# Feed-forward networks of a two-layer decoder as 2x2 blocks with seven products in place of eight

## The chip, the cores and the metric

The kernel runs on one core of one Trainium2 chip. The metric is device time in microseconds, from the first to the last instruction of the core, for one launch. TensorE (PE in the profile, PEld for its loading of the stationary side) multiplies matrices; VectorE (DVE), ScalarE (ACT) and GpSimd (POOL) work on elements; SyncE (SP) issues the transfers. Every engine takes its instructions in the order in which they stand in its own queue, and an instruction at the head that waits holds up all behind it.

## The reference

Two layers on 1024 tokens of 1024 values. Layer 0 mixes tokens by a gated delta rule, layer 1 by stick-breaking attention; behind each mixer stands a SwiGLU feed-forward network of 2816 columns. The change is in these two networks.

```python
def swiglu(x, w_gu, w_down):
    g, u = jnp.split(x @ w_gu, 2, axis=-1)
    return (jax.nn.silu(g) * u) @ w_down

    for layer in range(DEPTH):
        hn = rms_norm(h, attn_norm[layer])
        ...
        h = h + swiglu(rms_norm(h, ffn_norm[layer]), ffn_w_gu[layer], ffn_w_down[layer])
```

In float32. The kernel splits each side of a product into a high and a low part (float32r) and adds three products: high x high, high x low, low x high.

## The kernel before

The stream h lies in SBUF as eight tiles of 128 tokens x 1024. The tail of a mixer adds its output product to h by blocks (`final_put`, L329) and gives each finished row block to `Norm`: `tile` (L205 to L211) scales the row, `half` transposes half of the tokens (four 128x128 transposes a column block, L222) and splits the result to the high and low right sides `xT` (ACT L230, DVE L231). The first four row blocks are one half of the tokens, the other four the second half.

`ffn` (L334) goes over 22 column units of 128 columns, in groups of two or three. Of a unit, gate and up are two stationary matrices of 1024 x 128: `col_raw` (L111) loads one, 512 KB, `split` casts it (ACT, L102) and subtracts (DVE, L103). `proj_half` (L139 to L141) runs for each half of the tokens over 8 row blocks of the weights x 3 parts, 24 matmuls 128x512 into one PSUM bank. `gate` applies Silu (ACT, L344), `up` multiplies (DVE, L348) and splits the hidden values (ACT L351, DVE L352); these stay in SBUF. After a group, `row_unit` (L126) has loaded and split its rows of w_down, and `down_steps` (L256 to L258) makes the 16 blocks of 128 tokens x 512 columns, three matmuls a unit, each added to h by DVE (L329). In the first unit the products by the second half of the tokens wait for `norm.half()`, and the first half's stand ahead of it (`proj_two_steps`).

Loads are issued by SP in program order, as buffers come free (`raw` has 3, weights `w` 4). No order is written out by hand in these stages: program order is that of the code, and each engine waits only on the buffers and the data. The changed `ffn` below keeps the names of pools: `w` is the pool of weights in `main`, `n` the pool of row tiles with 4 buffers, `ips` and `ups` PSUM banks.

## Time and profile before

| | |
|---|---|
| time, median of 3 runs | 2762.84 us (2760.97 to 2763.07) |
| the profiled execution's own span | 2763.6 us, mean granted clock 0.996 |
| PE busy | 2691.2 us (97%), 13676 matmuls |
| DVE, ACT, POOL busy | 1392.3 (50%), 903.5 (33%), 531.2 (19%) |
| memory | 157.49 MB by the load and store queue, its packets 18.9% of 16 engines' time; 57 GB/s |
| layer 0's mixer, feed-forward | to 740, about 740 to 1460 |
| layer 1's mixer, feed-forward | about 1460 to 2050, 2050 to 2760 |

The span is that of one profiled execution and is 0.7 us above the median of the timed runs. Busy shares are averages over stages with different limits; what a stage is bound by is read from windows of that stage. A matmul of 512 columns shows a busy time of 0.39 us while the next starts 0.23 us later, since matmuls are pipelined: what one costs is the spacing of the starts.

### The profile page before, as it was taken

The numbers are of one execution on the slowest core, as the hardware profiler recorded it, in microseconds if no ns is written. First come the engines' busy times: TensorE is split into PE (matmuls) and PEld (weight loads), VectorE is DVE, ScalarE is ACT, GpSimd is POOL, SyncE is SP. The second block draws the span as 40 slices with busy tenths as digits, with TensorE's granted clock in tenths as the row PEclk, the third lists the DMA queues.
The fourth block names the chain that finished last, engine by engine and source line by source line (L and its number), as shares of the span: only waits on it lengthen the run. The fifth ranks groups of instructions, "written<-read, shape, count | busy, mean of one in ns | idle before, by whom it ended". The sixth has DMA issues, their size and how long they took to land.

```text
span 2763.6 us, 34344 instructions
## 1 busy us (share of the span) xinstructions
PE 2691.2 (97%) x13676; PEld 2216.1 (80%) x13676; DVE 1392.3 (50%) x2107; ACT 903.5 (33%) x1787; POOL 531.2 (19%) x1044
## 2 busy tenths in 40 slices
PE   8999999999999999999999999999899999999999
PEld 6787778877788888888887788887678888888887
DVE  6666677665633333232245787787743323223223
ACT  5333333342511121011135666667341112101211
POOL 2444444444200000000023334322400000000000
PEclk9999999999999999999999999999999999999999
DMA  4222222223111121121121111112311112102211
GB/s 121 58 63 63 55 61 53 70 93 111 58 50 39 46 69 46 31 61 54 31 99 39 39 31 39 39 47 88 119 38 46 47 38 69 54 23 61 62 28 72
DMA packets 182118, 159.67 MB, mean 58 GB/s; under 512 B 11443, under 2 KB 159038, under 8 KB 181958
## 3 DMA queue, kind: packets, MB, share of 16 engines
q1 hardware_dynamic: 181958, 157.49, 18.9%
q8 instruction: 107, 1.75, 0.3%
q14 instruction: 53, 0.43, 0.1%
HBM read 140.38 MB, written 17.07 MB: 57 GB/s over the span
## 4 chain that ended last, share of the span: by engine, by line
PE 77%; DVE 10%; ACT 4%; issue 4%; POOL 3%; DMA 2%; SPq 0%; POOLq 0%; DVEq 0%; ACTq 0%
PE ups L139 16%; PE ups L140 16%; PE ups L141 16%; PE ups L258 7%; PE ups L257 7%; PE ups L256 7%; DVE l L1005 2%; PE ips L535 2%; DVE wl L103 1%; ACT wh L102 1%; DVE y L502 1%; DMA raw<-in_w_kv_dram 1%; PE ips L222 1%; POOL raw L120 1%; DVE z L1006 1%
## 5 line engine op out<-in xcount | busy, mean ns | idle before, releaser
L139 PE MATMUL ups<-x,wh 128*128 128x512 f32 (+1 forms) x2320 | 936.9, 404 | 0.0
L141 PE MATMUL ups<-x,wl 128*128 128x512 f32 (+1 forms) x2320 | 911.4, 393 | 0.0
L140 PE MATMUL ups<-x,wh 128*128 128x512 f32 (+1 forms) x2320 | 908.1, 392 | 0.0
L141 PEld LDWEIGHTS ups<-x,wl 128*128 128x128 f32 (+1 forms) x2320 | 435.4, 188 | 92.3
L139 PEld LDWEIGHTS ups<-x,wh 128*128 128x128 f32 (+1 forms) x2320 | 436.4, 188 | 77.6
L140 PEld LDWEIGHTS ups<-x,wh 128*128 128x128 f32 (+1 forms) x2320 | 436.7, 188 | 76.1
L103 DVE TENSOR_TENSOR wl<-raw,wh 128x1024 fp32r<-128x1024 f32 x152 | 190.5, 1253 | 407.5 <-ACT wh L102 406.7
L329 DVE TENSOR_TENSOR h<-h,ups 128x512 f32<-128x512 f32 x256 | 175.0, 687 | 255.0 <-PE ups L258 254.9
L102 ACT CAST wh<-raw 128x1024 fp32r<-128x1024 f32 x152 | 159.7, 1051 | 396.4 <-PE ups L140 301.9
L256 PE MATMUL ups<-wdh,hidh 128*128 128x512 f32 x704 | 274.6, 390 | 0.0
L258 PE MATMUL ups<-wdh,hidl 128*128 128x512 f32 x704 | 274.1, 389 | 0.0
L257 PE MATMUL ups<-wdl,hidh 128*128 128x512 f32 x704 | 274.0, 389 | 0.0
L344 ACT ACTIVATE n<-ups 128x512 f32<-128x512 f32 x88 | 52.0, 591 | 517.6 <-PE ups L141 517.5
L120 POOL TENSOR_TENSOR raw<-raw,gains 128x256 f32<-128x256 f32 x96 | 77.6, 836 | 737.1 <-DMA raw<-in_w_kv_dram 709.6
L348 DVE TENSOR_TENSOR n<-n,ups 128x512 f32<-128x512 f32 x88 | 60.5, 688 | 267.2 <-PE ups L141 265.5
L258 PEld LDWEIGHTS ups<-wdh,hidl 128*128 128x128 f32 x704 | 132.2, 188 | 27.5
L257 PEld LDWEIGHTS ups<-wdl,hidh 128*128 128x128 f32 x704 | 132.2, 188 | 27.2
L256 PEld LDWEIGHTS ups<-wdh,hidh 128*128 128x128 f32 x704 | 132.2, 188 | 27.2
L502 DVE SCALAR_TENSOR_TENSOR y<-n,convc,y 128x512 f32<-128x512 f32 x144 | 112.8, 784 | 1.3
L351 ACT CAST hidh<-n 128x512 fp32r<-128x512 f32 x88 | 54.3, 618 | 149.5 <-DVE n L348 149.5
L1005 DVE TENSOR_TENSOR_SCAN l<-l 128x128 f32<-128x128 f32 (+3 forms) x64 | 89.2, 1394 | 22.6 <-POOL l L1001 22.6
L103 DVE TENSOR_TENSOR wdl<-raw,wdh 128x1024 fp32r<-128x1024 f32 x50 | 64.8, 1300 | 65.0 <-ACT wdh L102 65.0
(245 smaller groups left out, 3578.0 us busy)
## 6 DMA issues: line engine op xcount, KB each, us to landing
raw<-in_ffn_w_gu_dram SPq DMA_DIRECT2D x88, 512.0 KB, 3.9
raw<-in_ffn_w_down_dram SPq DMA_DIRECT2D x44, 512.0 KB, 3.5
raw<-in_gdn_w_in_dram SPq DMA_DIRECT2D x32, 512.0 KB, 4.2
ab<-adr SPq DMA_DIRECT2D x128, 64.0 KB, 2.7
raw<-in_w_kv_dram SPq DMA_DIRECT2D x16, 512.0 KB, 3.9
raw<-oT SPq DMA_DIRECT2D x15, 512.0 KB, 3.2
y<-in_x_dram SPq DMA_DIRECT2D x8, 512.0 KB, 7.6
gb<-gcd SPq DMA_DIRECT2D x16, 256.0 KB, 3.7
```

What stands on the lines that cost most here:

```text
L102: act.copy(hi, raw)
L103: dve.tensor_tensor(lo, raw, hi, op=ALU.subtract)
L120: pool.tensor_tensor(raw[:, ks], raw[:, ks], bc(gain[:, ks]), op=ALU.mult)
L139: pe.matmul(o, wh[:, kt, :m], xh, start=kt == 0, stop=False)
L140: pe.matmul(o, wh[:, kt, :m], xl, start=False, stop=False)
L141: pe.matmul(o, wl[:, kt, :m], xh, start=False, stop=kt == KT - 1)
L256: pe.matmul(ps, ah[:, sl], wh[:, ns], start=i == 0, stop=False)
L257: pe.matmul(ps, ah[:, sl], wl[:, ns], start=False, stop=False)
L258: pe.matmul(ps, al[:, sl], wh[:, ns], start=False, stop=i == n - 1)
L329: dve.tensor_tensor(hs, hs if acc is None else acc[t][nh], ps, op=ALU.add)
L502: dve.scalar_tensor_tensor(ys, xr[:, j + sl.start : j + sl.stop], w[j], ys, op0=ALU.mult, op1=ALU.add)
L1005: dve.tensor_tensor_scan(rv, rv, rv, 0.0, op0=ALU.add, op1=ALU.bypass)
```

## The change

Let x be split by halves of the tokens and of the 1024 inputs, and a network's weights alike, so that [C11 C12; C21 C22] = [A11 A12; A21 A22] [B11 B12; B21 B22] needs eight block products. The change computes it with seven, as in Winograd's form of Strassen's scheme, with sums of blocks before and after:

- `PairNorm` (in place of `Norm` ahead of the networks): of the second half of the tokens it makes the right sides T1 to T4 (differences with the first half, by POOL and DVE) and X22, of the first half X11 and X21.
- `Unit`: one column unit has gate and up as the two block rows. Its left sides are the four weight blocks g1, g2 (`split_g`, used in products 1 and 2), u2 (`split22`, product 4) and sums (`sum12`, `sum34` on POOL, for products 5, 6, 3, 7). `Seven.step` runs a product of 12 matmuls (`triple`, L446 to L448) into a bank and then the element work of it (`e1`, `c11`, ...). Products 3 and 4 of a unit follow product 1 of the next one (`ORDER`).
- the hidden values of two units are a 2x2 block of the next product's left side. `sums(q)` makes the sums of pair q on POOL, splits part of them, and `put` stores them to DRAM (`hsa` split, `hsb` as they are) in eleven stores of 256 KB, 512 bytes a piece. The first pair is stored without sums (`sums0`).
- `Right` and `Block`: w_down by pairs of units as right sides, with sums on POOL; the down products by groups of two pairs, seven products of 24 matmuls a block, a block being two tiles of 128 tokens. `Block.plain` makes the first pair by eight products. The sums go to h: by DVE from PSUM (`into`) or by an ACT copy and a POOL add (`via`).
- h is no longer held in SBUF during the column units: `keep_rows` stores its rows to `hmid` and `rows_load` fetches them ahead of the down blocks.

The core of the diff:

```diff
-    def ffn(h, norm, w_gu, w_down, hp, done):
...
-                    proj(norm.xT, col_unit(w_gu, i * P), gate)
-                    proj(norm.xT, col_unit(w_gu, FF + i * P), up)
...
-            run(down_steps(hid, ws, final_put(None, h, done if f == NF else lambda t, nh, ht: None)))
...
+        act.copy(hi, src)
+        dve.tensor_tensor(lo, src, hi, op=ALU.subtract)
+        return hi, lo
...
+            rr = [self.hp.tile([P, 2, HB], F32, tag="W", name="r2", bufs=NW) for _ in range(4)]
+            tt = []
+            for j in range(4):
+                r = rr[j]
+                act.activation(r[:, 0], self.columns(hn, j), AF.Copy, scale=g(j))
+                t1, t2 = x_tile(F32), x_tile(F32)
+                pool.tensor_tensor(t1, r[:, 0], self.raw[j], op=ALU.subtract)
+                act.activation(r[:, 1], self.columns(hn, 4 + j), AF.Copy, scale=g(4 + j))
+                dve.tensor_tensor(t2, r[:, 1], t1, op=ALU.subtract)
+                tt.append((t1, t2))
+            for j in range(4):
+                self.parts("T2", j, tt[j][1])
+            for j in range(4):
+                pool.tensor_tensor(rr[j][:, 0], rr[j][:, 1], rr[j][:, 0], op=ALU.subtract)
+                self.parts("T1", j, tt[j][0])
+            for j in range(4):
+                self.parts("T3", j, rr[j][:, 0])
+                pool.tensor_tensor(rr[j][:, 0], self.raw[4 + j], tt[j][1], op=ALU.subtract)
+            for j in range(4):
+                self.parts("22", j, rr[j][:, 1], self.x2)
+            for j in range(4):
+                self.parts("T4", j, rr[j][:, 0])
...
+        ORDER = (1, -3, -4, 6, 2, 5, 7)
...
+            key, start = {1: ("B", True), 6: ("B", False), 7: ("B", False), 4: ("B", False),
+                          2: ("A", True), 5: ("C", True), 3: ("C", False)}[p]
+            if start:
+                self.bank[i, key] = i_tile((P, HB)) if key == "B" else u_tile()
+            ps = self.bank[i, key]
+            it.products(p, ps, start, p in (2, 3, 4))
+            if p == 2 and not out:
+                return
+            {1: it.e1, 2: it.c11, 6: it.u2, 5: it.p5, 7: lambda q: it.u3(q, self.bank[i, "C"]),
+             4: it.c21, 3: it.c12}[p](ps)
...
+            return hp.tile([P, 2, 4, P], dt, tag="W", name="w", bufs=NW)
...
+            def sum12(self):
+                self.s = W()
+                pool.tensor_tensor(self.s[:, 0], self.u[:, 0], self.u[:, 1], op=ALU.add)
+                pool.tensor_tensor(self.s[:, 1], self.s[:, 0], self.g[:, 0], op=ALU.subtract)
+            def sum34(self):
+                self.r = W()
+                pool.tensor_tensor(self.r[:, 0], self.g[:, 0], self.u[:, 0], op=ALU.subtract)
+                pool.tensor_tensor(self.r[:, 1], self.g[:, 1], self.s[:, 1], op=ALU.subtract)
...
+            def split12(self):
+                self.both(5, 6, self.s, W)
...
+            def split_g(self):
+                self.both(1, 2, self.g, mw)
...
+            def e1(self, ps):
+                self.t1 = ev()
+                act.copy(self.t1, ps)
...
+            def c11(self, ps):
+                self.sg = n_tile()
+                s = self.sg[:, 0:HB]
+                dve.tensor_tensor(s, self.t1, ps, op=ALU.add)
+                act.activation(s, s, AF.Silu)
...
+            def u2(self, ps):
+                self.t2 = ev()
+                act.copy(self.t2, ps)
...
+            def u3(self, ps, c):
+                self.t3 = ev()
+                act.copy(self.t3, ps)
+                dve.tensor_tensor(self.t3, self.t3, c, op=ALU.add)
...
+            def c21(self, ps):
+                s = self.sg[:, 0:HB]
+                dve.tensor_tensor(s, s, ps, op=ALU.mult)
...
+            def c12(self, ps):
+                s = self.sg[:, HB:S]
+                dve.tensor_tensor(s, self.t2, ps, op=ALU.add)
+                act.activation(s, s, AF.Silu)
+                pool.tensor_tensor(s, s, self.t3, op=ALU.mult)
...
+        def put(dst, k, src):
+            sp.dma_start(dst[:, :, k, :].rearrange("c p x -> p c x"), src)
...
+            v = [hid.pop(2 * q + k) for k in range(2)]
+            s = W()
+            pool.tensor_tensor(s[:, 0], v[0][:, :, 1], v[1][:, :, 1], op=ALU.add)
+            pool.tensor_tensor(s[:, 1], s[:, 0], v[0][:, :, 0], op=ALU.subtract)
+            yield
+            r = W()
+            pool.tensor_tensor(r[:, 0], v[0][:, :, 0], v[0][:, :, 1], op=ALU.subtract)
+            pool.tensor_tensor(r[:, 1], v[1][:, :, 0], s[:, 1], op=ALU.subtract)
+            put(hsb[q], 1, v[1][:, :, 1])
+            yield
+            hi = mw()
+            act.copy(hi, s)
+            dve.tensor_tensor(s, s, hi, op=ALU.subtract)
+            put(hsb[q], 0, r[:, 0])
+            put(hsb[q], 2, r[:, 1])
+            yield
+            h2 = mw()
+            for k in range(2):
+                act.copy(h2[:, k], v[k][:, :, 0])
+                dve.tensor_tensor(v[k][:, :, 0], v[k][:, :, 0], h2[:, k], op=ALU.subtract)
+            for k in range(2):
+                put(hsa[q], 2 + k, hi[:, k].bitcast(F32))
+                put(hsa[q], 6 + k, s[:, k])
+            yield
+            for k in range(2):
+                put(hsa[q], k, h2[:, k].bitcast(F32))
+                put(hsa[q], 4 + k, v[k][:, :, 0])
...
+        def rows_load(c):
+            for t in (2 * c, 2 * c + 1):
+                sp.dma_start(h[t], rows[t * P : (t + 1) * P, :])
...
+            def via(self, ps, odd, nh):
+                e = ev()
+                act.copy(e, ps)
+                d = self.half(odd, nh)
+                pool.tensor_tensor(d, d, e, op=ALU.add)
+            def into(self, ps, odd, nh):
+                d = self.half(odd, nh)
+                dve.tensor_tensor(d, d, ps, op=ALU.add)
...
+            def e1(self, ps):
+                self.into(ps, 0, 0)
+            def c11(self, ps):
+                self.into(ps, 0, 0)
+                self.finish(0, 0)
+            def u2(self, ps):
+                self.via(ps, 0, 1)
+            def p5(self, ps):
+                self.into(ps, 1, 1)
+            def u3(self, ps, c):
+                self.via(ps, 1, 1)
+                self.finish(1, 1)
...
+            elif s == 2:
+                if j:
+                    j.split22()
+            elif s == 3:
+                if j:
+                    j.sum34()
+                    if i + 2 < NF:
+                        units[i + 2].load_u()
+                if i % 2 == 0 and i >= 2:
+                    pend.append(sums(i // 2 - 1) if i > 2 else sums0())
+            elif s == 5:
+                if j:
+                    j.split_g()
+            elif s == 6:
+                if j:
+                    j.split12()
+                    if i + 2 < NF:
+                        units[i + 2].load_g()
...
+        run_.step(0, 1)
+        run_.step(0, 2, False)
+        units[1].load_g()
+        units[1].split22()
+        units[1].split_g()
+        run_.step(1, 1)
+        run_.step(1, 2, False)
+        norm.half()
+        for i in range(2):
+            units[i].c11(run_.bank[i, "A"])
+        units[1].sum12()
+        run_.step(0, 6)
+        units[1].sum34()
+        units[2].load_u()
```

Where the instructions stand at the three places that the numbers of the prediction rest on:

PE at the entry of the first network, before: the last transposes of the second half (`n` are the scaled row tiles, `ident` the identity), then the first products by that half (`x` its right sides, `wh` and `wl` the first unit's gate).

```order
L222 MATMUL ips_7748<-ident_69,n_7579 128x128
L222 MATMUL ips_7748<-ident_69,n_7619 128x128
L139 MATMUL ups_7766<-x_7699,wh_7628 128x512 [waits Activation_49]
L222 MATMUL ips_7757<-ident_69,n_7499 128x128 [waits DVE_49]
L222 MATMUL ips_7757<-ident_69,n_7539 128x128
L222 MATMUL ips_7757<-ident_69,n_7579 128x128
L222 MATMUL ips_7757<-ident_69,n_7619 128x128
L140 MATMUL ups_7766<-x_7700,wh_7628 128x512
L141 MATMUL ups_7766<-x_7699,wl_7629 128x512
L139 MATMUL ups_7766<-x_7708,wh_7628 128x512 [waits Activation_49]
L140 MATMUL ups_7766<-x_7709,wh_7628 128x512
L141 MATMUL ups_7766<-x_7708,wl_7629 128x512
```

The same place after the change: the last transposes of the second half, then product 6 of unit 0 (`w` its left side, `x` the right side T2).

```order
L378 MATMUL ips_7827<-ident_69,n_7506 128x128 [waits Activation_49]
L378 MATMUL ips_7827<-ident_69,n_7552 128x128
L378 MATMUL ips_7827<-ident_69,n_7598 128x128
L378 MATMUL ips_7827<-ident_69,n_7644 128x128
L446 MATMUL ips_7701<-x_7834,w_7688 128x512 [waits Activation_49]
L447 MATMUL ips_7701<-x_7835,w_7688 128x512 [waits DVE_49]
L448 MATMUL ips_7701<-x_7834,w_7689 128x512
L446 MATMUL ips_7701<-x_7838,w_7688 128x512 [waits Activation_49]
L447 MATMUL ips_7701<-x_7839,w_7688 128x512 [waits DVE_49]
L448 MATMUL ips_7701<-x_7838,w_7689 128x512
```

The right sides behind the transposes come now from POOL and DVE differences as well; the row blocks' transposes wait for ACT, and each triple of product 6 waits for ACT and DVE.

ACT in a group of column units of the first network, before: `wdh` and `wh` are high parts of weights, `hidh` those of hidden values, `n` the Silu.

```order
L344 ACTIVATE n_9296<-ups_9303 128x512 [waits PE_49]
L102 CAST wh_9618<-raw_9616 128x1024 [waits DMAHW1_49,PE_49,Activation_49]
L344 ACTIVATE n_9296<-ups_9329 128x512 [waits PE_49]
L351 CAST hidh_9387<-n_9296 128x512 [waits DVE_49]
L102 CAST wh_9676<-raw_9674 128x1024 [waits DMAHW2_49,PE_49,Activation_49]
L351 CAST hidh_9417<-n_9296 128x512 [waits DVE_49]
L344 ACTIVATE n_9615<-ups_9622 128x512 [waits PE_49]
L102 CAST wh_9743<-raw_9741 128x1024 [waits DMAHW3_49,PE_49,Activation_49]
```

ACT in an even column unit after the change: `ips` holds the bank of products 1, 6 and 7; the cast of w_9213 (`split12` of the next unit) waits for transfers and POOL, and the cast from raw_9336 and the copy L538 (`u3`) stand behind it.

```order
L521 COPY ev_9211<-ips_9198 128x512 [waits PE_49,Pool_49]
L549 ACTIVATE n_9157<-n_9157 128x512 [waits DVE_49]
L531 COPY ev_9265<-ips_9198 128x512 [waits PE_49]
L358 CAST w_9332<-w_9213 128x1024 [waits DMAHW1_49,DMAHW0_49,Pool_49]
L583 CAST w_9312<-w_9272 128x1024 [waits PE_49]
L527 ACTIVATE n_9288<-n_9288 128x512 [waits DVE_49]
L590 CAST w_9338<-n_9007 128x512 [waits DMAHW7_49,PE_49]
L590 CAST w_9338<-n_9157 128x512
L358 CAST w_9369<-w_9267 128x512 [waits DVE_49,Activation_49]
L358 CAST w_9454<-raw_9336 128x1024 [waits DMAHW3_49,DMAHW5_49,DMAHW2_49,Activation_49]
L538 COPY ev_9329<-ips_9198 128x512 [waits PE_49]
```

Of the casts before, none waits for a store; now `split12` takes a buffer (tag W) that the stores of the pair's sums read.

SP at the passage from column units to down products of the first network, before: loads of the next weights, each as a `raw` buffer comes free.

```order
L111 DMA raw_9297<-in_ffn_w_gu_dram 128x8x128 [waits DMAHW1_49,DVE_49]
L111 DMA raw_9355<-in_ffn_w_gu_dram 128x8x128 [waits DMAHW2_49,DVE_49]
L126 DMA raw_9421<-in_ffn_w_down_dram 128x1024 [waits DMAHW3_49,DVE_49]
L126 DMA raw_9427<-in_ffn_w_down_dram 128x1024 [waits DMAHW6_49,DVE_49]
L126 DMA raw_9433<-in_ffn_w_down_dram 128x1024 [waits DMAHW4_49,DVE_49]
L111 DMA raw_9616<-in_ffn_w_gu_dram 128x8x128 [waits DMAHW7_49,DVE_49]
```

The same queue after the change: the last stores of the last pair, then the loads of the third block's left sides (`hsa` from DRAM, into w_11028 and w_11074).

```order
L553 DMA hsa_7660<-w_10982 128x4x128 [waits DMAHW1_49]
L553 DMA hsa_7660<-w_10953 128x4x128 [waits DMAHW2_49]
L553 DMA hsa_7660<-w_11007 128x4x128 [waits DMAHW3_49,Activation_49]
L553 DMA hsa_7660<-n_10691 128x4x128 [waits DMAHW4_49,DVE_49]
L553 DMA hsa_7660<-w_11007 128x4x128 [waits DMAHW5_49,Activation_49]
L553 DMA hsa_7660<-n_10852 128x4x128 [waits DMAHW6_49,DVE_49]
L664 DMA w_11028<-hsa_7650 128x1024 [waits DMAHW7_49,PE_49]
L687 DMA h_11032<-hmid_7294 128x1024 [waits DMAHW0_49]
L664 DMA w_11074<-hsa_7650 128x1024 [waits DMAHW1_49]
L687 DMA h_11076<-hmid_7294 128x1024 [waits DMAHW2_49]
```

The loads of the third block's left sides stand behind eleven stores that wait for the sums of the last pair.

## Rows read from the trace of the kernel before

**Rows 1.** The page: its head, and busy time, share and instructions of each engine.

```profile
span 2763.6 us, 34344 instructions
PE 2691.2 (97%) x13676; PEld 2216.1 (80%) x13676; DVE 1392.3 (50%) x2107; ACT 903.5 (33%) x1787; POOL 531.2 (19%) x1044
```

**Rows 2.** Busy time of a stretch inside a network; columns are in the first line.

```profile
core 0: us, PE busy (x) PEld busy (x) DVE busy (x) ACT busy (x) POOL busy (x), PEclk, DMA share, GB/s
900.00:1100.00 200.00, 200.00 (x884) 165.69 (x883) 61.42 (x77) 33.22 (x44) 0.00 (x0) 1.00 0.18 53
```

**Rows 3.** Groups by form: busy us, mean ns of one, idle before by releaser.

```profile
L612 POOL TENSOR_TENSOR qd<-y,gb 128x512 f32<-128x512 f32 x16 | 20.7, 1291 | 75.8 <-DVE y L505 38.0 <-PE ips L689 37.1 <-ACT sz L513 0.7
L329 DVE TENSOR_TENSOR h<-h,ups 128x512 f32<-128x512 f32 x256 | 175.0, 687 | 255.0 <-PE ups L258 254.9
L352 DVE TENSOR_TENSOR hidl<-n,hidh 128x512 fp32r<-128x512 f32 x88 | 60.9, 692 | 21.3 <-ACT hidh L351 21.3
L102 ACT CAST wh<-raw 128x1024 fp32r<-128x1024 f32 x152 | 159.7, 1051 | 396.4 <-PE ups L140 301.9 <-issue 85.7 <-DMA raw<-in_ffn_w_gu_dram 5.4
L351 ACT CAST hidh<-n 128x512 fp32r<-128x512 f32 x88 | 54.3, 618 | 149.5 <-DVE n L348 149.5
L344 ACT ACTIVATE n<-ups 128x512 f32<-128x512 f32 x88 | 52.0, 591 | 517.6 <-PE ups L141 517.5
```

**Rows 4.** Single lines: duration ns min/median/max, first and last start us, form.

```profile
L103 DVE TENSOR_TENSOR wl<-raw,wh x152: 1197/1226/2315, 17.6 to 2706.4; 128x1024 fp32r<-128x1024 f32 x152
L321 POOL TENSOR_TENSOR x<-x,n x32: 1277/1301/2298, 675.2 to 1982.9; 128x512 f32<-128x512 f32 x32
L309 DVE TENSOR_TENSOR x<-x,ups x64: 649/686/691, 640.4 to 2007.9; 128x512 f32<-128x512 f32 x64
```

**Rows 5.** The page: transfers, KB each, median us from issue to landing.

```profile
y<-in_x_dram SPq DMA_DIRECT2D x8, 512.0 KB, 7.6
hsp<-h SPq DMA_DIRECT2D x8, 512.0 KB, 2.6
n<-hsp SPq DMA_DIRECT2D x8, 512.0 KB, 3.3
out_dram<-h SPq DMA_DIRECT2D x16, 256.0 KB, 2.0
```

**Rows 6.** Timeline of PE at a network's entry: start, us, instruction, idle before it.

```profile
740.67 3.48 PE L222 MATMUL ips<-ident,n 128*128 128x128 f32 x28
743.90 0.48 PE L139 MATMUL ups<-x,wh 128*128 128x512 f32 x1
744.22 0.60 PE L222 MATMUL ips<-ident,n 128*128 128x128 f32 x4
```

**Rows 7.** Timelines of DVE and of POOL in the mixer's tail, 696 to 701.8.

```profile
696.61 4.30 DVE L103 TENSOR_TENSOR wdl<-raw,wdh 128x1024 fp32r<-128x1024 f32 x2 [0.67 <-ACT wdh L102]
...
697.54 2.29 POOL L321 TENSOR_TENSOR x<-x,n 128x512 f32<-128x512 f32 x1
```

**Rows 8.** Timeline of PE behind two gaps, and the first one's window.

```profile
701.61 0.68 PE L256 MATMUL ups<-wdh,x 128*128 128x512 f32 x1 [2.31 <-issue]
...
702.51 0.63 PE L258 MATMUL ups<-wdh,x 128*128 128x512 f32 x1
702.94 0.63 PE L256 MATMUL ups<-wdh,x 128*128 128x512 f32 x1
...
1972.87 0.50 PE L256 MATMUL ups<-kh,x 128*128 128x512 f32 x1 [2.39 <-DVE x L309]
...
1973.44 0.39 PE L258 MATMUL ups<-kh,x 128*128 128x512 f32 x1
1973.67 0.40 PE L256 MATMUL ups<-qh,x 128*128 128x512 f32 x1
...
700.00:720.00 20.00, 17.74 (x76) 14.28 (x77) 14.59 (x20) 10.18 (x14) 7.96 (x11) 0.91 0.44 130
```

**Rows 9.** The page: the queue's packets, bytes, share of 16 engines' span.

```profile
q1 hardware_dynamic: 181958, 157.49, 18.9%
```

More of the change, by code (lines that the diff above doesn't have):

```diff
@@ new lines, in yoco_kernel, with __init__, x2, columns @@
+    class PairNorm(Norm):
+        def __init__(self, gain, hp):
+            super().__init__(gain)
+            self.hp = hp
+            self.X = {n: [None] * 4 for n in ("11", "21", "T1", "T2", "T3", "T4", "22")}
+            self.raw, self.nhalf = {}, 0
+        def x2(self, dt=F32R):
+            return self.hp.tile([P, HB], dt, tag="x2", name="x2", bufs=NX2)
+        def columns(self, hn, kt):
+            ps = i_tile()
+            for j in range(NTH):
+                pe.transpose(ps[:, j, :], hn[j][:, kt * P : (kt + 1) * P], ident)
+            return ps.rearrange("p a b -> p (a b)")
+        def parts(self, name, j, src, tile_=None):
+            tile_ = x_tile if tile_ is None else tile_
+            self.X[name][j] = parts_of(src, tile_(), tile_())
+        def half(self, n=KT):
+            g = lambda kt: self.gain[:, kt : kt + 1]
+            if self.nhalf == 0:
+                if not self.todo:
+                    self.todo, self.hn = [(self.hn, kt) for kt in range(KT)], []
+                for hn, kt in self.todo[:n]:
+                    r = self.x2(F32)
+                    act.activation(r, self.columns(hn, kt), AF.Copy, scale=g(kt))
+                    self.raw[kt] = r
+                    self.parts(("11", "21")[kt // 4], kt % 4, r, self.x2)
+                self.todo = self.todo[n:]
+                if not self.todo:
+                    self.nhalf = 1
+                return
+            hn, self.hn = self.hn, []
+            rr = [self.hp.tile([P, 2, HB], F32, tag="W", name="r2", bufs=NW) for _ in range(4)]
[20 more added lines that the diff above has]
+                self.parts("T4", j, rr[j][:, 0])
```

380 lines of the change are left out of this document (348 added, 32 removed).

## The prediction

> **What bounds the kernel now.** I read the page first for the shares of the engines: TensorE (PE) is busy for 2691.2 of 2763.6 us [rows 1]. Then the table by stretches, inside the feed-forward networks, which run at about 745 to 1460 and 2050 to 2760: there PE has no idle time at all, at a granted clock of 1.00, with 884 matmuls in 200 us [rows 2], so 0.2262 us a matmul. VectorE (DVE) is busy for 61 of these 200 us, ScalarE (ACT) for 33, GpSimd (POOL) for none. So the networks are bound by the number of matmuls and nothing else. The change takes matmuls away and lays other work on the three idle engines; the sum is what is taken, less what PE then waits for.
>
> **What is taken.** A network holds 22 column units x 2 (gate, up) x 48 = 2112 matmuls for gate and up and 22 x 48 = 1056 for down, 3168. After the change a column unit is seven products of 12 matmuls, so 22 x 84 = 1848; of down, the first pair of units takes eight products (96), the five groups of two pairs take 168 each (840): 2784. That is 384 fewer in a network, 768 in both. The moving side stays 512 wide, so at 0.2262 us this is 173.7 us. All of it lay on the path. The floor, with no new wait, is 2763.6 - 173.7 = 2589.9 us.
>
> **What is added, by engine.** POOL has no 128x512 operation in these stages; the nearest row is L612, 1.29 us. A DVE operation with PSUM is 0.687 us (L329) and with SBUF alone 0.69 (L352); an ACT copy is taken as L344's 0.59, casts are 0.62 (L351) and 1.05 (L102, twice as wide); a wide DVE subtraction is 1.23 [rows 3, 4]. For two column units, 168 matmuls or 38.0 us of PE, this gives POOL 14 x 1.29 = 18 us, DVE 17, ACT 16. For a group of four down blocks, again 38.0 us, DVE has 20 adds from PSUM (13.7) and 13.9 us of subtractions in SBUF, POOL 16 operations (20.6). None exceeds PE. So a loss arises only where one of these queues stands in the wrong order for a moment. I looked for such places in the order of the instructions and found four.
>
> **1. Entry of the network.** Before, the second half's 32 transposes and the first product by it follow one another without a gap [rows 6]. Afterwards that half passes through 12 POOL subtractions and 24 DVE ones before all seven right sides are there. Only four products (10.9 us) need the first half alone. Two parts: (a) the second unit's first product waits for a cast that stands eighth in ACT's queue, behind five casts of 0.62, one of 1.05 and a copy of 0.59, and takes 1.05 itself: 5.8, about 6 us; at best 0, if the casts run while PE is still in the mixer. (b) DVE's 24 subtractions, two adds and a weight's subtraction are 24 x 0.69 + 2 x 0.69 + 1.23 = 19.2 us if POOL (15.5 us) disturbs none of them, 34.7 if every one; PE reaches the sixth product, which needs the last of them, after 13.6 us. So 6 to 21 us, and I take 13, since at most half of POOL's operations can meet them. Entry: 19, between 6 and 27.
>
> **2. Steady column units.** In an even unit, the unit's number being i, the left sides of the pair before are added on POOL, then stored. The chain from the unit's start: PE ends the product that is needed at 5.4 us, DVE 0.7, ACT 0.6, POOL 1.3 for the last hidden values, then four POOL sums of 1.29: 13.6 us with the small gaps between engines. The last two sums are stored from a buffer that the next unit's 1024-wide cast on ACT wants again. A store of 256 KB lands after 2.0 us, one of 512 KB after 2.6 [rows 5]; with 2.4, since these come in small pieces, the cast starts at 16.0. Behind it in ACT's queue stand 5.6 us of casts and then the copy that DVE's sum of two banks needs; with DVE's 0.69 and the gaps this is there at 23.5 us. PE wants to add into that bank at 19.0 + 2.7 = 21.7. So 1.8 us, up to 3.3 if the cast's own 1.05 and the stores of both queues come one after the other; I take 2.3. Nine pairs make 21. At the lowest 0, where PE is already late for another reason; at the highest 30.
>
> **3. From units to down blocks.** The loads of the third block's left sides stand behind the last pair's eleven stores in SP's queue, and these wait for that pair's sums. The sums end 32 to 35 us after the last unit begins, the stores are issued and the load then takes 3.3 us [rows 5], against 19.0 for the unit and two blocks by eight products of 5.4 us each. That is late by 4 to 7 us; I take 5. If nothing were late there it would be 0.
>
> **4. Down blocks.** Half of the sums of a block go by DVE, two by an ACT copy and a POOL add. DVE's subtractions in SBUF and POOL's operations together are 34.5 of the 38.0 us. Where they meet, they are slow: in a stretch of the mixer's tail a POOL subtraction of 1.30 us took 2.29, and two DVE subtractions 4.30 instead of 2.45 [rows 7]; over the program L103 goes from 1.226 to 2.315 and L321 from 1.30 to 2.30, while L309, which reads PSUM, never goes over 0.691 [rows 4]. So the two wait for one another in SBUF, and not where DVE reads PSUM. I take 1 us a group, 5 in all, between 0 and 51 (below). The Trainium skill says the same of the cause in "SBUF — State Buffer", section "Who interferes with whom": an operation of GpSimd and one of VectorE with two SBUF inputs hold a shared pair of ports exclusively, and an operation with one SBUF input doesn't. By that rule POOL's and DVE's times add up strictly; it is the third case below.
>
> **5. Clock.** After a gap of 2.31 us the next eight matmuls stand 0.43 us apart, not 0.23: the granted clock of that stretch falls to 0.91, with part of it at 1.2 GHz, the lower level, and the eight lose 8 x 0.2 = 1.6 us. After another gap, of 2.39 us, the spacing is 0.23 at once [rows 8]. So one gap pays and another does not. In a network the new waits make nine of about 2 us and some four longer ones, 26 in both; with 1 us for 10 of them I add 10, between 0 and 26 x 1.6 = 42. The Trainium skill, "TensorE: Matmul & The Clock Gate", section "HAM oscillation — how this bites in real kernels", says that a loop which waits in every turn pays the slow clock in every turn. By that all 26 would pay, some 42 us, or 2732 in place of 2700; the row of the unpunished gap speaks against it.
>
> **Nothing is charged** for the memory traffic. The left sides (2.9 MB a pair, stored and loaded) and the rows of h add about 140 MB to 157; that queue's packets took 18.9% of the engines' time [rows 9], so about 36% afterwards. Nor for the outputs: the last add and a 2.0 us store end the program as before.
>
> **Sum.** 2763.6 - 173.7 + 2 x (19 + 21 + 5 + 5) + 10 = 2699.9 us of span; the median of the runs is 0.7 below the span, so 2699, which I give as 2700.
>
> **Rivals.**
> First, **PE stays the bound** and the seams are hidden. For it: each engine has under half of PE's time in units, and lateness at one seam absorbs that of the next (a late PE finds the stores landed). Against it: the cast that waits for a store is in each of the nine even units, in one in-order queue. With an entry of 14 in both networks, 5 for the clock and nothing else: 2763.6 - 173.7 + 28 + 5 - 0.7 = 2622.
> Second, **DVE and POOL become the bound in the down blocks.** If each POOL operation stops DVE, whose queue is in order, so that the adds from PSUM wait too, a group takes 13.7 + 13.9 + 20.6 = 48.2 us, not 38.0: 10.2 too much, in ten groups 102. With half of that, and the other terms as above, 2700 + 51 - 10 = 2741. For it: the row of 4.30 us. Against it: POOL can run while DVE adds from PSUM, 13.7 us of each group, and L309 was never slowed.
> Third, **slower than before**, by one mechanism: the stores that hold the cast's buffer land late. They are written in pieces of 512 bytes, and no row of before stores in that form; the longest landing in before is 7.6 us for 512 KB [rows 5], in a crowd of loads. Each 1 us of landing is 1 us of wait in each even unit, 18 in both networks. The losses beside it are 2 x 29 + 10 = 68, so the gain is gone when the 18 waits together reach 173.7 - 68 = 106 us, or 5.9 each, which is a landing of 2.4 + 3.6 = 6.0 us in every unit. At 7.0 it is 2700 + 18 x 4.6 = 2783. Against it: landings of 2.0 and 2.6 us for the stores in before, and the queue's share [rows 9].
> That the matmuls are not fewer is excluded: the order of the changed program has 1856 each of L446, L447 and L448.
>
> **Chances.** The forecast (2665 to 2735) has 0.48, the hidden seams (2600 to 2665) 0.28, the bound by DVE and POOL (2735 to 2757) 0.16, slower 0.08. A measurement of this kernel can tell some 0.2%, 5.5 us, from no change. Of the third case 0.03 ends within that. So faster 0.89, same 0.03, slower 0.08. The range of 8 in 10 goes from 2625, which leaves out half of the hidden seams' lower part, to 2745.
>
> **What would show it.** PE busy should fall by about 160 to 174 us, with 768 fewer matmuls. Steps 1 to 4 are right where PE idles 12 to 25 us behind the second half's transposes, about 2 us in each even unit just before the third product, with the copy L538 the last to come, 4 to 7 us before the third block, and next to nothing in the later blocks. Wrong: no wait at L538 (hidden seams), DVE subtractions of over 2 us throughout the down blocks (second rival), stores L553 that land after 5 us (third). The entry is the term I trust least.

## The result: 49 us slower, where 63 us faster was forecast

The changed kernel takes 2811.95 us (median of 4 runs, 2811.56 to 2815.18) against 2762.95 us before: ratio 1.0176, 95% interval 1.0162 to 1.0191. The forecast was 2700, with 2625 to 2745 as range. The profiled execution has a span of 2810.5 us.

The page of the changed kernel, head and engines (busy us, share, instructions), to be read against [rows 1]:

```profile
span 2810.5 us, 35880 instructions
PE 2580.1 (92%) x12908; PEld 2096.4 (75%) x12908; DVE 1716.2 (61%) x2491; ACT 1209.5 (43%) x2359; POOL 1218.3 (43%) x1536
```

The matmuls fell from 13676 to 12908, 768 as counted. PE busy fell by only 111 us, where the prediction had 160 to 174, since many of the matmuls left stand farther apart (below), and PE is now idle for 230 us where it was 72. By stages (columns in the first line): the entry of the first network, its steady column units, the passage to the down blocks, and the down blocks.

```profile
core 0: us, PE busy (x) PEld busy (x) DVE busy (x) ACT busy (x) POOL busy (x), PEclk, DMA share, GB/s
732.00:807.00 75.00, 48.62 (x190) 35.68 (x188) 48.12 (x51) 41.56 (x68) 44.35 (x34) 0.82 0.18 56
830.00:1209.00 379.00, 353.87 (x1512) 289.19 (x1510) 154.21 (x188) 136.49 (x208) 163.69 (x122) 0.97 0.40 116
1240.00:1256.00 16.00, 5.52 (x19) 4.18 (x18) 9.99 (x13) 3.32 (x8) 7.85 (x5) 0.68 0.96 309
1256.00:1456.00 200.00, 186.18 (x795) 150.42 (x795) 148.08 (x191) 75.60 (x136) 107.64 (x82) 0.98 0.56 191
```

Before, a stretch of a network was 200.00 of 200.00 us PE at clock 1.00 [rows 2]. Now every stage has idle time and a granted clock below 1.00. None of the three other engines is full in any of them: in the steady units DVE, ACT and POOL are busy for 41, 36 and 43% of the time. The 16 DMA engines are full in one, the passage, for 0.96 of its time.

What PE waited for, over the whole program (us in total, times, longest us):

```profile
PE ups L446 <- DVE ev L539: 57.8, 22, 4.1
PE ups L446 <- DMA w<-hsa: 20.4, 2, 10.5
PE ups L446 <- DVE h L728: 17.6, 13, 3.0
PE ips L447 <- DVE x L359: 17.4, 6, 7.3
PE ips L446 <- ACT w L358: 12.7, 4, 5.4
PE ips L446 <- DVE h L728: 10.8, 6, 2.1
PE ups L446 <- ACT x L358: 8.9, 4, 2.2
```

These are the four places that the prediction named: L539 in the units, `hsa` at the passage, L728 in the blocks, the others (and two of the waits at L539) at the entry. I measured what each stage lost by taking from its length the number of its matmuls x 0.2263 us, and 3.7 us for the entry's 32 transposes, which were there before too (28 in 3.23 us, [rows 6]). First network, without its last group of blocks, where the next mixer's work stands between: entry 38, units 39, passage 12, blocks 20, together 109; second network: 38, 36, 12, 20, together 106. The 215 us, less the 173.7 us taken away, are 41 of the 47 us by which the span grew. Of the first network's 109, idle time before a matmul is 77 (entry 27, units 26, passage 10, blocks 14), in 32 gaps; the other 32 are matmuls that came slower. In the second network 76 and 30. Of these 62 us of both networks, 31 stand in 153 matmuls that begin 0.40 to 0.46 us after the one before, which is the lower of the clock's two levels, 1.2 GHz: the stretch of 953 to 959 us, behind such a gap, has a granted clock of 0.72. The other half is mostly what each restart costs at either level: the second matmul behind a gap comes 0.34 us after the first even where the rest are 0.23 apart, and idle time counts only from the end of a matmul's 0.39 us.

**One steady unit, and its chain.** Timelines of the changed kernel's SP, POOL, ACT, DVE and PE in an even unit whose first product began at 972.0 (start, us, instruction, idle before it and what ended it):

```profile
983.77 2.97 SPq L553 DMA_DIRECT2D hsb<-w  x2
...
985.06 1.29 POOL L579 TENSOR_TENSOR w<-n,w 128x512 f32<-128x512 f32 x1
...
988.75 1.05 ACT L358 CAST w<-w 128x1024 fp32r<-128x1024 f32 x1 [5.06 <-DMA hsb<-w]
989.71 1.05 ACT L583 CAST w<-w 128x1024 fp32r<-128x1024 f32 x1
990.66 0.62 ACT L527 ACTIVATE n<-n 128x512 f32<-128x512 f32 x1
991.19 1.13 ACT L590 CAST w<-n 128x512 fp32r<-128x512 f32 x2
993.57 0.62 ACT L358 CAST w<-w 128x512 fp32r<-128x512 f32 x1 [1.26 <-DVE w L359]
994.17 1.05 ACT L358 CAST w<-raw 128x1024 fp32r<-128x1024 f32 x1
995.13 0.58 ACT L538 COPY ev<-ips 128x512 f32<-128x512 f32 x1
...
995.74 0.69 DVE L539 TENSOR_TENSOR ev<-ev,ups 128x512 f32<-128x512 f32 x1 [0.45 <-ACT ev L538]
...
996.48 0.80 PE L446 MATMUL ups<-x,w 128*128 128x512 f32 x1 [2.54 <-DVE ev L539]
...
998.36 0.63 PE L447 MATMUL ups<-x,w 128*128 128x512 f32 x1
998.78 0.63 PE L448 MATMUL ups<-x,w 128*128 128x512 f32 x1
```

The last sum ends at 14.3 us into the unit, its store (the second of the two in the first row) lands and the cast starts at 16.7, the copy L538 ends at 23.7 and PE goes on at 24.5: within 1 us of the chain in step 2. The last two rows are what step 2 did not hold: behind the gap the matmuls stand 0.42 us apart.

**The passage.** Timelines of SP and PE of the same kernel, and the issue times on SP of the stores (duration ns min/median/max):

```profile
1240.19 3.64 SPq L553 DMA_DIRECT2D hsa<-w  x5
...
1246.74 0.83 SPq L664 DMA_DIRECT2D w<-hsa  x1
...
1252.53 0.77 PE L446 MATMUL ups<-wd,w 128*128 128x512 f32 x1 [10.48 <-DMA w<-hsa]
```

```profile
L553 SPq DMA_DIRECT2D hsa<-w x128: 359/534/883, 800.8 to 2576.4; - x128
L553 SPq DMA_DIRECT2D hsa<-n x48: 359/820/1432, 801.9 to 2577.3; - x48
```

The load stands behind the stores, and PE waits 5.8 us from its issue on. The transfers of this stage fill the DMA engines (0.96 of the time in the table above, 309 GB/s), which fits a load that takes 5.8 us; no run here separates that from the rest.

**One wait in the down blocks**, the same kernel, ACT, POOL, DVE and PE:

```profile
1352.33 0.62 ACT L358 CAST x<-w 128x512 fp32r<-128x512 f32 x1 [2.21 <-POOL w L639]
...
1354.42 0.62 ACT L358 CAST wd<-w 128x512 fp32r<-128x512 f32 x1
...
1356.42 0.68 DVE L359 TENSOR_TENSOR wd<-w,wd 128x512 fp32r<-128x512 f32 x1
...
1357.18 1.68 POOL L640 TENSOR_TENSOR w<-raw 128x512 f32<-128x512 f32 x1 [3.63 <-DVE wd L359]
...
1358.89 0.63 ACT L358 CAST x<-w 128x512 fp32r<-128x512 f32 x1 [3.38 <-POOL w L640]
...
1359.55 1.10 DVE L359 TENSOR_TENSOR x<-w,x 128x512 fp32r<-128x512 f32 x1 [1.25 <-ACT x L358]
1360.58 1.75 DVE L359 TENSOR_TENSOR x<-n,x 128x512 fp32r<-128x512 f32 x1
1362.25 0.68 DVE L728 TENSOR_TENSOR h<-h,ups 128x512 f32<-128x512 f32 x1
...
1362.98 0.50 PE L446 MATMUL ups<-wd,x 128*128 128x512 f32 x1 [2.91 <-DVE h L728]
```

A cast of the next pair (x<-w) stands in ACT's queue ahead of the last cast of the pair before (wd<-w) and waits for POOL; POOL's next sum waits for the buffer which that last cast and its subtraction would free; ACT's next cast waits for that sum and DVE's subtraction for the cast, and the add L728, for which PE's bank waits, stands behind it. Two of the subtractions ahead of the add take 1.10 and 1.75 us, where 0.69 is the time of one alone: beside a GpSimd sum of 1.71 in the same microseconds. So the order and the slowing meet in this wait; the slowing is some 1.5 us of it.

### The profile page after: what moved, and what is told of

It is laid out like the page before. It is cut to its first block, busy times and chain, and to the rows that moved or that the text cites. A ratio compares the mean times of both kernels' runs of the same rounds, so it can differ in the third digit from the quotient of the medians.

```text
span 2810.5 us, 35880 instructions
## 1 busy us (share of the span) xinstructions
PE 2580.1 (92%) x12908; PEld 2096.4 (75%) x12908; DVE 1716.2 (61%) x2491; ACT 1209.5 (43%) x2359; POOL 1218.3 (43%) x1536
## 5 line engine op out<-in xcount | busy, mean ns | idle before, releaser
L139 PE MATMUL ups<-x,wh 128*128 128x512 f32 (+1 forms) x912 | 388.9, 427 | 0.0
L141 PE MATMUL ups<-x,wl 128*128 128x512 f32 (+1 forms) x912 | 363.6, 399 | 0.0
L140 PE MATMUL ups<-x,wh 128*128 128x512 f32 (+1 forms) x912 | 359.7, 395 | 0.0
L446 PE MATMUL ips<-x,w 128*128 128x512 f32 x792 | 313.6, 396 | 25.1 <-ACT w L358 12.7
L447 PE MATMUL ips<-x,w 128*128 128x512 f32 x792 | 313.2, 395 | 17.4 <-DVE x L359 17.4
L448 PE MATMUL ips<-x,w 128*128 128x512 f32 x792 | 311.7, 394 | 2.5 <-DVE w L359 2.5
L446 PE MATMUL ups<-x,w 128*128 128x512 f32 x600 | 248.4, 414 | 66.7 <-DVE ev L539 57.8
L447 PE MATMUL ups<-x,w 128*128 128x512 f32 x600 | 244.7, 408 | 1.6 <-DVE x L359 1.6
L448 PE MATMUL ups<-x,w 128*128 128x512 f32 x600 | 242.9, 405 | 0.0
L141 PEld LDWEIGHTS ups<-x,wl 128*128 128x128 f32 (+1 forms) x912 | 170.9, 187 | 37.7
L446 PEld LDWEIGHTS ips<-x,w 128*128 128x128 f32 x792 | 151.3, 191 | 61.2 <-ACT w L358 15.0
L446 PEld LDWEIGHTS ups<-x,w 128*128 128x128 f32 x600 | 119.0, 198 | 102.9 <-DVE ev L539 67.5
L724 POOL TENSOR_TENSOR h<-h,ev 128x512 f32<-128x512 f32 x88 | 123.6, 1405 | 166.3 <-ACT ev L722 159.0
L447 PEld LDWEIGHTS ips<-x,w 128*128 128x128 f32 x792 | 151.4, 191 | 51.4 <-DVE x L359 20.2
L139 PEld LDWEIGHTS ups<-x,wh 128*128 128x128 f32 (+1 forms) x912 | 172.2, 189 | 22.7
L140 PEld LDWEIGHTS ups<-x,wh 128*128 128x128 f32 (+1 forms) x912 | 172.2, 189 | 21.2
L448 PEld LDWEIGHTS ips<-x,w 128*128 128x128 f32 x792 | 150.6, 190 | 35.0 <-DVE w L359 3.9
L447 PEld LDWEIGHTS ups<-x,w 128*128 128x128 f32 x600 | 119.5, 199 | 28.0 <-DVE x L359 3.2
L359 DVE TENSOR_TENSOR w<-w 128x1024 fp32r<-128x1024 f32 x132 | 121.7, 939 | 27.6 <-ACT w L358 27.6
```

The costliest lines, as they stand in the source:

```text
L139: pe.matmul(o, wh[:, kt, :m], xh, start=kt == 0, stop=False)
L140: pe.matmul(o, wh[:, kt, :m], xl, start=False, stop=False)
L141: pe.matmul(o, wl[:, kt, :m], xh, start=False, stop=kt == KT - 1)
L359: dve.tensor_tensor(lo, src, hi, op=ALU.subtract)
L446: pe.matmul(ps, ah, bh, start=start, stop=False, skip_group_check=True)
L447: pe.matmul(ps, ah, bl, start=False, stop=False, skip_group_check=True)
```

## The experiments

Two theories were put against each other. **A**: each wait is one instruction that stands in the wrong place of an in-order queue, and PE's clock falls behind it; undone, its loss comes back. **B**: VectorE and GpSimd are crowded (they slow one another in SBUF), so PE will wait elsewhere once one wait is gone. All edits are to the changed kernel; the ratios are to the kernel before, which ran beside them (2764.1 to 2764.3 us).

**The wait in the units, by buffer.**

```diff
-            r = W()
-            pool.tensor_tensor(r[:, 0], v[0][:, :, 0], v[0][:, :, 1], op=ALU.subtract)
-            pool.tensor_tensor(r[:, 1], v[1][:, :, 0], s[:, 1], op=ALU.subtract)
             put(hsb[q], 1, v[1][:, :, 1])
+            pool.tensor_tensor(v[0][:, :, 1], v[0][:, :, 0], v[0][:, :, 1], op=ALU.subtract)
+            pool.tensor_tensor(v[1][:, :, 1], v[1][:, :, 0], s[:, 1], op=ALU.subtract)
...
-            put(hsb[q], 0, r[:, 0])
-            put(hsb[q], 2, r[:, 1])
+            put(hsb[q], 0, v[0][:, :, 1])
+            put(hsb[q], 2, v[1][:, :, 1])
```

> The last two sums of a pair are written over the hidden values that are no longer needed, not into a new buffer, so no cast of the next unit's weights waits for their store. Theory A (each wait is one instruction in the wrong place of a queue, and PE's clock falls after it): the wait before product 3 in each even unit goes, 23.6 us of idle and some 9 to 14 us of slow clock in a network, so 2812 - 2 x 30 to 37 = 2738 to 2752. Theory B (VectorE and GpSimd are crowded, so PE waits elsewhere once this wait is gone): less than 25 us, 2787 or more.

Measured: 2750.27 us, ratio 0.9947 (0.9929 to 0.9965), 62 us less than the changed kernel. In the first network the units lose 4 us in place of 39.

**The same wait, by order alone.**

```diff
-                act.copy(self.t3, ps)
+                self.c3 = act.copy(self.t3, ps)
...
                 if j:
-                    j.split12()
+                    with tc.issue_after(u.c3.ins):   # u.c3: the copy of product 7
+                        j.split12()
```

> All buffers as in the changed kernel; the 1024-wide cast of the next unit's weights is queued on ScalarE behind the copy of product 7. It waits for the same stores, but the copy no longer does. Theory A: about the same gain as with the sums in place, 2738 to 2755. If the late landing of the store itself were the cause, the cast would be late for product 6 of the next unit and the wait only moves: 2800 to 2812. Theory B: 2787 or more.

Measured: 2745.97 us, ratio 0.9930 (0.9911 to 0.9948), 66 us less. The cast still waits for the stores, and nothing else does. The units' window, and what PE still waits for at L539 over the program (57.8 before the edit):

```profile
830.00:1209.00 379.00, 373.45 (x1646) 308.42 (x1644) 177.84 (x215) 145.80 (x229) 199.34 (x140) 1.00 0.48 143
```

```profile
PE ups L446 <- DVE ev L539: 8.1, 5, 3.4
```

The clock is back at 1.00 and 134 more matmuls fit in the same 379 us. That is theory A, and the place in the queue, not the landing of the store, is the cause: with VectorE and GpSimd busier than before (178 and 199 us), nothing moved elsewhere in the units.

**The clock by itself.** Twelve matmuls that nobody reads, in each even unit where PE waits:

```diff
                 if i > 1:
                     u.split3()
+                if i % 2 and i >= 5:
+                    dummy = i_tile((P, HB))
+                    u.products(1, dummy, True, True)
```

> The changed kernel with twelve more matmuls, read by nobody, in each even unit (from the fourth) at the place where PE waits 2.5 us before product 3; 9 x 12 in a network, 2.72 us each time. Clock theory (the wait is followed by 1.5 us at the lower clock in 6 of 9 units): the idle time is used up by work and the slow clock goes: 2 x 9 x (2.72 - 2.6) + 0 - 2 x 6 x 1.5 = 2812 - 16 = 2796. Rival (the matmuls behind the wait are slow for another reason, or PE's own work holds up what it waits for): the added work costs what it takes or the wait stays, 2812 to 2860.

Measured: 2798.87 us, ratio 1.0125 (1.0101 to 1.0148): 216 matmuls more, 48.9 us of work, and 13 us less time (by the two intervals, 5 to 21). The same window and the same wait:

```profile
830.00:1209.00 379.00, 377.05 (x1657) 310.23 (x1656) 161.03 (x193) 139.06 (x212) 167.22 (x124) 1.00 0.42 124
```

```profile
PE ups L446 <- DVE ev L539: 11.2, 9, 3.4
```

The chain that PE waited for is left as it was; the useless work only fills its time. PE's wait at L539 falls by 46.6 us, 2.3 less than the work put in. So some 15 us, 0.9 a gap, are what the lower clock and the restarts took behind these 18 gaps, with the uncertainty of the 13. The traces say the same: the granted clock of the window is 1.00 in place of 0.97, and of the 67 matmuls that stood 0.40 to 0.46 us apart in the units of the two networks, 13 us in all above the usual spacing, one is left.

**The entry.**

```diff
+        norm.half()
         run_.step(1, 1)
         run_.step(1, 2, False)
-        norm.half()
...
-                pool.tensor_tensor(rr[j][:, 0], rr[j][:, 1], rr[j][:, 0], op=ALU.subtract)
+                with tc.issue_after(last.ins):       # last: the fourth difference for T1
+                    pool.tensor_tensor(rr[j][:, 0], rr[j][:, 1], rr[j][:, 0], op=ALU.subtract)
```

> At a network's entry the second half's transposes stand ahead of the second unit's first two products, and GpSimd makes the four differences for products 5 and 6 before those for product 7. Theory A: the entry lost 39.8 us in the first network, of which 7.3 in one wait for VectorE and 5.4 for ScalarE; 5.4 us of PE's work now lie beside the chain and 5 us of GpSimd's come later, so 8 to 15 us a network with the clock, 2782 to 2796. Theory B: under 8 us in all, 2804 or more.

Measured: 2786.04 us, ratio 1.0079 (1.0060 to 1.0098), 26 us less. What is left shows on DVE and POOL of this kernel:

```profile
771.52 6.79 DVE L359 TENSOR_TENSOR x<-r,x 128x512 fp32r<-128x512 f32 x4 [2.39 <-POOL r L418]
...
770.23 4.15 POOL L418 TENSOR_TENSOR r<-x,x 128x512 f32<-128x512 f32 x3
774.35 1.72 POOL L488 TENSOR_TENSOR w<-raw 128x512 f32<-128x512 f32 x1
776.03 1.72 POOL L489 TENSOR_TENSOR w<-raw,w 128x512 f32<-128x512 f32 x1
```

Four subtractions at 1.7 us each on VectorE (0.69 alone), and 1.72 for one GpSimd operation (1.29 alone): here the two go in step, as theory B has it. Of the 38 us that the first network's entry loses, order alone gives back 10.

**The last pair's sums later.**

```diff
-                if b == 0 and s == 2:
+                if b == 1 and s == 2:
                     pend.append(sums(NPAIR - 1))
```

> The sums and stores of the last pair are made one down block later, so that the loads of the third block's left sides stand ahead of the eleven stores. Theory A: the wait of 10.5 us and 1.5 us of slow clock behind it go in each network, 2812 - 24 = 2788. Theory B: the same work falls into the next blocks, where VectorE is fuller, and comes back there: 2800 or more.

Measured: 2810.50 us, ratio 1.0167 (1.0146 to 1.0187): no change that can be told from the changed kernel's 1.0176. The wait for the load was replaced. DVE and PE of this kernel:

```profile
1242.23 2.30 DVE L584 TENSOR_TENSOR w<-w 128x1024 f32<-128x1024 f32 x1 [3.06 <-POOL w L579]
1244.46 1.27 DVE L728 TENSOR_TENSOR h<-h,ups 128x512 f32<-128x512 f32 x2
...
1245.19 0.80 PE L446 MATMUL ups<-wd,w 128*128 128x512 f32 x1 [4.36 <-DVE h L728]
```

The sums came hardly later than before (the first of them on GpSimd at 1235.0 us, where it was 1233.4), though the call stands a whole block later. So the order of a queue is not that of the code alone, as the section on the kernel before has it; that the program's scheduler goes by what it takes to be ready is my reading. The subtraction of the sums, which waits for GpSimd, now stood ahead of the adds L728. That row is the mechanism of theory A, but the time is what theory B expected (2800 or more), my 24 us were wrong, and moving the call was no test between the two.

**The blocks' queues in the order of the program**, with the last pair's sums called one block later:

```diff
+    def queued(key, fn, *a, **k):        # behind the last one queued so on this engine
+        if key in last:
+            with tc.issue_after(last[key].ins):
+                last[key] = fn(*a, **k)
...
-                dve.tensor_tensor(d, d, ps, op=ALU.add)
+                queued("d", dve.tensor_tensor, d, d, ps, op=ALU.add)
```

(the same for the copies of `via`, the casts and subtractions of `Right.split`, `hid_split` and the last pair's sums)

> The changed kernel with the element work of the down blocks and of the last pair's sums queued on ScalarE and VectorE in the order in which the program is written, and these sums one block later. Theory A (a subtraction that waits for GpSimd stands ahead of the adds from PSUM): 17 us at the passage and some 15 of the 22 us in the blocks go in each network, 2812 - 2 x 25 to 32 = 2748 to 2762. Theory B (VectorE and GpSimd slow one another there; their SBUF work is 34.5 of 38 us): the order changes little, 2795 or more.

Measured: 2780.04 us, ratio 1.0062 (1.0041 to 1.0083), 32 us less, where A said 50 to 64 and B under 17. In the first network the first group of two pairs loses 3.6 us and each of the next three 1.2, in place of some 19 for the four. So the order is enough in the blocks, though the slowing that B names is there too: of VectorE's 512-wide subtractions in SBUF in the first network's blocks 36 of 71 took over 1 us in the changed kernel, and 16 of 73 here. It fell short at two places that the order itself made: the fifth block's load still stood behind the stores (5.3 us), and in the last group the next mixer's row scaling waited in the same queues:

```profile
PE ips L460 <- DMA w<-hsa: 10.5, 2, 5.3
PE ips L222 <- DVE n L211: 9.4, 3, 4.7
```

**GpSimd relieved.** The two sums of a block that went by copy and GpSimd, by VectorE from PSUM:

```diff
-                e = ev()
-                act.copy(e, ps)
                 d = self.half(odd, nh)
-                pool.tensor_tensor(d, d, e, op=ALU.add)
+                dve.tensor_tensor(d, d, ps, op=ALU.add)
```

> The changed kernel with the two sums of each down block that went by a ScalarE copy and a GpSimd add now added by VectorE from PSUM. GpSimd loses 8 of its 16 operations a group, VectorE gets 5.5 us more from PSUM. Theory B: the SBUF work of both falls from 34.5 to 24 us of 38 and most of the 22 us lost in the blocks of each network goes: 2768 to 2785. Theory A: the sums on GpSimd come somewhat earlier, so a part of it, but VectorE's queue is fuller: 2795 to 2815.

Measured: 2788.28 us, ratio 1.0089 (1.0066 to 1.0111), 24 us less, between the two expectations. This alone doesn't separate them: less work on GpSimd makes its sums earlier in either theory. The experiment before does: with GpSimd's whole work in place, order alone brought the groups down to 1.2 us.

**Units and entry together.** The edits of the second and the fourth experiment.

> The cast behind the copy and the early second half together. Theory A: the two lie in different stages and add: 2812 - 66 - 26 = 2720, within 8. Theory B (crowding): the second gives less once the first is made: 2730 to 2746.

Measured: 2727.77 us, ratio 0.9863 (0.9841 to 0.9885). 84 us less, 92 would be the plain sum: they add, just within the 8 us.

**All orders in one kernel**: sums in place, cast behind the copy, early second half, blocks in order except in the first network's last group, and

```diff
+                    if b == 0:
+                        hid_load(1)
+                        hid_load(2)
+                        rows_load(1)
+                        hid_load(3)
...
-                if b == 0 and s == 2:
+                if b == 1 and s == 0:
                     pend.append(sums(NPAIR - 1))
```

> All undone waits in one kernel: sums of a pair in place, the cast behind the copy, the early second half, the down blocks' element work in program order (not in the first network's last group, where it held up the next mixer's rows by 4.7 us), and the loads of the second to fourth block's left sides ahead of the last pair's stores. If the waits are separate, the gains add: 2812 - 66 (units) - 26 (entry) - 32 (blocks and passage) - 2 x 5 (the passage's rest) - 2 x 5 (the first network's last group, once) = 2673 to 2690. If crowding is behind them, they overlap and 2700 or more remains.

Measured: 2678.30 us, ratio 0.9687 (0.9672 to 0.9701): 3.1% faster than the kernel before, with the same 12908 matmuls and the same element work as the slower kernel. Its page, and the units' window:

```profile
span 2674.2 us, 35863 instructions
PE 2547.2 (95%) x12908; PEld 2079.2 (78%) x12908; DVE 1714.6 (64%) x2491; ACT 1190.7 (45%) x2359; POOL 1239.4 (46%) x1536
```

```profile
830.00:1209.00 379.00, 376.65 (x1659) 310.49 (x1658) 182.66 (x221) 146.67 (x233) 201.40 (x139) 1.00 0.50 153
```

In the first network the loss up to the last group is now 40 us: 29.6 at the entry, 1.7 in the units, 2.6 at the passage, 6.5 in the blocks.

**The first differences by VectorE**, on top of it:

```diff
-                last = pool.tensor_tensor(t1, r[:, 0], self.raw[j], op=ALU.subtract)
+                dve.tensor_tensor(t1, r[:, 0], self.raw[j], op=ALU.subtract)
```

> As the kernel with all orders, and the four first differences of the second half made by VectorE, not by GpSimd. In the kernel with the early second half they took 1.6 us each on GpSimd, beside VectorE operations that took 1.7 in place of 0.69. If the two slowing one another sets the entry's length, products 5 and 6 are ready 3 us earlier and the entry is 3 to 6 us shorter in each network: 6 to 12 us below the other kernel. If the order in ScalarE's and VectorE's queues sets it, four more operations in VectorE's queue bring nothing or cost up to 5 us in all.

Measured: 2675.31 us, ratio 0.9682 (0.9665 to 0.9699), not to be told from the kernel with all orders. The edit also drops the order behind `last`, which pointed at the operations moved. In the first network it is 4.9 us ahead when the first 156 matmuls have begun and 0.4 after 240: products 5 and 6 are earlier, the wait at L539 (3.42 us, 0.51 in the other) takes 2.9 of it back, and matmuls 0.43 us apart behind that wait take 1.6. In the second network, where both kernels wait 3.4 us at L539, 2.7 us remain. What bounds the remaining 30 us of the entry is not settled; a GpSimd operation moved is not enough.

## Why the prediction was wrong

**The floor was right.** 768 matmuls fewer, and 2.72 us for twelve in each stretch without a wait, as taken.

**1, entry: the term was mis-sized.** 19 taken, 6 to 27 as bounds, 38 measured, of which 27 are idle time, the upper bound, and 11 belong to step 5. Part (a), the four products of the first half, lost 11, of which 6 are idle time, as taken, but by luck: the wait that the step named, for the cast of the second unit, was 0.9 us, and 5.2 were waits for unit 0's own right sides (2.2 and 2.2 of them for ScalarE), which the step did not have. Part (b) lost 27, of which 21 are idle time, the upper bound of the step. Its 13 rested on "at most half of POOL's operations can meet them"; 8 of GpSimd's 12 differences took 1.7 to 1.8 us, and 8 of VectorE's 24 subtractions 1.5 to 1.8. The step also had no order on GpSimd: the largest wait, 7.3 us in product 6, stands behind VectorE's fourth difference, which needs GpSimd's fourth one for T1, and in GpSimd's queue these alternate with differences that only product 7 needs. With those behind, and the half earlier, the wait was 2.5.

**2, units: the mechanism was right, and its idle time to a fifth.** 2.3 us a pair were taken, 2.4 to 2.9 are seen in eight of the first network's nine and 4.1 in one, 25 us in all for 21. The rest of the 39 is the clock and the restart behind each gap. The landings, which I bounded from rows of another form of store, were 2.3 us for the stores that hold the buffer (ten of forty can be followed to their landing), as taken.

**3, passage: mis-sized.** 5 taken, 10.5 measured (and 1.5 of clock). The load was issued 43 us after the last unit's begin, where the step had the sums end at 32 to 35 and the stores issued at no cost: VectorE ended the last of them at 40.6, the stores hold SP for 0.36 to 1.4 us each, and the load took 5.8 us, not 3.3. A second error hid part of it: PE came to the third block at 38.3 us, not 29.8, mostly since the step left out products 3 and 4 of the last unit, 24 matmuls or 5.4 us, which stand in the first block's turn.

**4, blocks: mis-sized, and for a reason that the step did not name.** 5 taken, 20 measured, 14 of them idle time. I looked for slowing in SBUF; it is there (up to 1.78 us in place of 0.69), but the wait is a subtraction ahead of an add in VectorE's queue, an order which I had found in the units' ScalarE queue and did not look for here.

**5, clock: the term that failed most.** 10 us taken for both networks, 62 measured, of which 31 are matmuls at the lower clock; the restart behind each gap, the most of the other half, was put at nothing without a reason. I set 1 us for 10 of 26 gaps, after one gap in [rows 8] that cost nothing. There were 32 gaps in a network, and in the first network's units six of the nine show the spacing of 0.42 behind them, in the second's four. The sum by the page "TensorE: Matmul & The Clock Gate" of the Trainium skill, section "HAM oscillation — how this bites in real kernels", in which each turn of a loop pays, would have been 42; that section speaks of a loop whose waits are longer than most of the gaps here, which the prediction did not say. The trace agrees with it in part: gaps of 2.5 to 4.1 us paid again and again, but 8 of the 18 show full speed at once.

**The rivals.** The third had the sign, and its place, the buffer held by the stores, is the largest wait in total. But its condition, a landing of 6 us, did not hold: the stores landed as taken, and the sum of all seams decided. The sign came true by another way than the one it named. The second's slowing was found at the entry and in the blocks (half of the 512-wide subtractions there over 1 us), but not the 2 us and more throughout that it was to show, and in the blocks the order alone brought most of the time back. The rule of "SBUF — State Buffer" in the Trainium skill, section "Who interferes with whom", agrees with the rows in what it names: the two slow one another with two inputs in SBUF, while the adds from PSUM in the blocks never go over 0.69 us. The prediction took from it that the times add up strictly; they do not quite: in step, one operation of each took 1.7 us, where 0.69 and 1.29 make 1.98. The first, hidden seams at 2622, was not reached by the kernel with all orders either: its 2678 is nearer to the forecast.

In one sentence: 173.7 us were taken and 215 came back, as 153 us of waits (100 forecast) and 62 of slower matmuls (10 forecast, for the clock alone).

## What to carry to other kernels

When work is taken off a bound engine and laid on idle ones, their busy shares say nothing of the time: read their queues at each seam, for every engine, for an instruction that waits for something far away with a short, urgent one behind it. Price each gap of the matmul engine with its idle time and the clock behind it, and charge the issuing queue for each store. Here edits of order and buffers alone, with the same arithmetic, turned 1.8% slower into 3.1% faster.

## What the runs showed of the hardware

Filling a gap with matmuls that nobody reads made the program faster: 216 more, 13 us less, and a granted clock of 1.00 in place of 0.97. VectorE and GpSimd, both with two inputs in SBUF and their operations back to back, go in step at 1.7 us an operation, where alone they take 0.69 and 1.29. A store of 256 KB in pieces of 512 bytes held SP's queue for 0.36 us where it stood alone, from a strided tile (`hsb<-n`, 0.37) as from a whole one (`hsb<-w`, 0.37); right behind another it took longer, 0.6 to 0.8 us at the median and up to 1.43.
